# Encoder trunk on one core: norm and rotation of q and k for both token tiles at once on paired PSUM banks, key copies by DMA, attention-weight copies on ScalarE, the first norm in a set order

## The chip, the core and the metric

The kernel runs on one core of one Trainium2 chip. The metric is the device time in microseconds (us), a median over runs; less is better. TensorE (PE) does matmuls and transposes, VectorE (DVE) and ScalarE (ACT) work elementwise and read PSUM, GpSimd (POOL) does small elementwise work on SBUF, SyncE (SP) issues DMAs.

## The reference

Two layers of an encoder trunk on 256 tokens of 1024 channels, float32. Each layer projects the normed input once to the q, k, v of four mixers and four gates, mixes, and runs a convolutional feed-forward block:

```python
for l in range(DEPTH):                                   # DEPTH = 2
    h = rms_norm(x, norm1_g[l])
    aq, ak, av, bq, bk, bv, cq, ck, cv, dq, dk, dv, g = split_parts(h @ w_in[l])   # 12544 columns
    aq = rope(rms_norm(aq, gq[0, 0]), ang_1d)            # per head of 64: norm, gain, rotation
    ak = rope(rms_norm(ak, gq[0, 1]), ang_1d)
    o_a = diff_attention(aq, ak, av, ...)                # A: differential, dense
    ...                                                  # B: grouped queries, axial rotation
    ...                                                  # C: three dilated windows, 1-D rotation
    dq = rms_norm(dq, gq[3, 0]); dk = rms_norm(dk, gq[3, 1])
    o_d = neighbourhood_attention(dq, dk, dv, rpb[l])    # D: with position bias, no rotation
    merged = sum(gate[:, :, i] * (o_i @ w_branch[l, i]) for i, o_i in enumerate(mixers))
    x = x + merged @ w_out[l]
    x = x + conv_ffn(rms_norm(x, norm2_g[l]), w_up[l], conv_w[l], conv_b[l], w_down[l])
```

## The kernel before

The 256 tokens are two tiles of 128 partitions, t = 0 and 1. Weights stream in as jobs of 1 MB (`load`, L261, on SP's queue, three jobs ahead). `split` makes each half job a high and a low part: ScalarE casts (`hi`, L272), VectorE subtracts (`lo`, L273). A product is three matmuls (L346 to L348: hi x hTh, lo x hTh, hi x hTl; L342 to L344 with the weights stationary), so that two parts of the activations (`hTh`, `hTl`) and of the weights give nearly float32.

A block of 512 output columns is two jobs; a block of `branch` and the smaller `bkv` (kB) are one. The blocks follow a list: `qD kB kD qB kA vD qA vA gD0 kC1 kC0 qC1 bD0 gD1 vC0 qC0 qC2 bD1 kC2 vC1 vC2 gB0 bB0 ...` (q, k, v, g for gates, b for branches; A to D are the mixers). Each block holds two PSUM banks, one for each token tile, out of four buffers of the tag `mm`; a buffer is given to a later block when all that read it are done.

`run` walks through the jobs in quarters, and `at(j, q, fn)` hangs other work on quarter q of job j. All is put down as a program; the framework's scheduler then fixes each engine's order of instructions by a timeline of its own, with the earlier program place as the priority. `behind(ins)` lets what it encloses come after `ins` on the same engine.

What the change touches:

- `qk_vec` (L452 on), after the last quarter of a q or k block, once for each tile: ScalarE squares out of PSUM (L457), VectorE sums by head (L460), GpSimd adds the epsilon (L161) and takes the power -0.5 (L162), VectorE multiplies out of PSUM (L463, which frees the bank), and, except for D, rotates in SBUF (L479 twice or four times, L480, L482). The square's buffer `sq` is a single one, shared with the end of mixer A (`finish`, L677 to L682).
- `tr_k` (L758 on): transposes the keys of kA and kC0 (L488) and writes four operands, each with both partition halves, by four ScalarE copies (L767) and four VectorE subtractions (L769) for each tile. The dense scores read them at L527.
- `transp` (L601 on): transposes the weights of an attention unit (L608) and copies them out of PSUM on VectorE (L614); the weighted sum of mixer A is L646.
- `norm_vec`, `norm_tr` (L412, L420, L434, L437): the norm's scaling, its transposes and the copies to `hTh` and `hTl`.
- `neigh_bias` (L223): four bias matmuls for each tile half, fed by 16 loads of `rpb` on SP's queue in each layer.
- `first_norm` (L1118 on): x, the first weights and the gain row are loaded; TensorE runs 16 warm-up matmuls on zeros (L1143), then spreads the gain row over the partitions (L1149).
- `layouts` (L316 to L329): 18 matmuls on zeros behind the last product, whose result nothing reads.

Of the kernel before, what the change touches and what calls it, by code (L numbers as in the profile page):

```python
# [10 lines left out]
F32 = mybir.dt.float32  # L11
# [75 lines left out]
class Trunk:  # L87
# [77 lines left out]
    def prologue(self, l):  # L165
        nc = self.nc
        qkg = self.sb(self.tp, "qn", [128, 512], F32, bufs=3).rearrange("p (m k d) -> p m k d", m=4, k=2)
        nc.sync.dma_start(qkg, self.dram("qk_g", l * 512, [[0, 128], [1, 512]]))
        lam = self.sb(self.tp, "t2", [128, 512], F32, bufs=1)[:, :256].rearrange("p (a d) -> p a d", a=4)
# [113 lines left out]
    def run(self):  # L283
        for j in range(1, LOAD_AHEAD):
            self.load(j)
        for i in range(1, 3):
            self.split(i)
# [25 lines left out]
        with self.behind((self.last_mm,)):  # L313
            self.layouts()

    def layouts(self):  # L316

        z = self.sb(self.wp, "hi", [128, 1024], F32R, bufs=5)
        self.nc.gpsimd.memset(z[:].bitcast(F32), 0.0)
        b = self.sb(self.tp, "e", [128, 1024], mybir.dt.bfloat16, bufs=3)  # L320
        self.nc.gpsimd.memset(b, 0.0)
        p = self.ps("mm")
        v = z[:]
        at = lambda off, *dims: bass.AP(v.tensor, v.offset + off, [v.ap[0], *dims])
        kinds = [(z[:, :128], at(0, (1, 512))), (z[:, :128], at(8, (1, 512))), (z[:, :128], at(8, (0, 256), (1, 2))),
                 (z[:, :128], at(8, (16, 32), (1, 16))), (z[:, :128], at(0, (2, 512))), (b[:, :128], b[:, :512])]
        for w, m in kinds:
            for i in range(3):
                self.nc.tensor.matmul(p, w, m, start=i == 0, stop=i == 2)  # L329
# [55 lines left out]
    def in_block(self, l, col0, tile_major=False):  # L385
# [3 lines left out]
        def out():  # L389
            if "o" not in cell:  # L390
                cell["o"] = [self.ps("mm"), self.ps("mm")]
            return cell["o"]
# [8 lines left out]
    def norm_vec(self, t, g, ss, n):  # L401
# [7 lines left out]
        xn = self.t4([128, DM])  # L409
        for i in range(2):  # L410
            s = slice(i * 512, (i + 1) * 512)
            nc.vector.scalar_tensor_tensor(xn[:, s], self.x[:, t, s], rs[:, 0:1], g[i] if isinstance(g, list) else g[:, s], op0=ALU.mult, op1=ALU.mult)  # L412
        return xn

    def norm_tr(self, t, xn, by_token=False, halves=(0, 1)):

        for i in halves:
            p = self.ps("mm")
# [23 lines left out]
    def sumsq(self, t, cols, ss, i, vector=False):  # L442
        junk = self.sb(self.tp, "t2" if vector else "sq", [128, 512], F32, bufs=1)
# [8 lines left out]
    def qk_vec(self, p, t, m, k, nh, res):  # L452
# [3 lines left out]
        sq = self.sb(self.tp, "sq", [128, 512], F32, bufs=1)  # L456
        nc.scalar.activation(sq[:, :w], p[:, :w], AF.Square, scale=0.125)  # L457
        rs = self.small("qr", 8)
        hv = lambda a: a.rearrange("p (h d) -> p h d", d=64)
        nc.vector.tensor_reduce(rs[:, :nh], hv(sq[:, :w]), AX.X, ALU.add)  # L460
        self.rsqrt_mean(rs[:, :nh], rs[:, :nh], nh)
        qn = self.sb(self.tp, "qn", [128, 512], F32, bufs=3)
        nc.vector.tensor_tensor(hv(qn[:, :w]), hv(p[:, :w]), rs[:, :nh].unsqueeze(2).to_broadcast([128, nh, 64]), ALU.mult)  # L463
        if m == MD:
            if k == 1:
                nc.vector.tensor_tensor(hv(qn[:, :w]), hv(qn[:, :w]),
                                        self.dtab.unsqueeze(1).to_broadcast([128, nh, 64]), ALU.mult)
        else:
            t2 = self.sb(self.tp, "t2", [128, 512], F32, bufs=1)
            hw = 16 if m == MB else 32  # L470
            rv = lambda a: a.rearrange("p (h b w) -> p h b w", b=2, w=hw)
            tv = lambda a: a.rearrange("p (a b w) -> p a b w", b=2, w=hw)
            na = 64 // (2 * hw)
            for a in range(na):
                for b in range(2):
                    o = t2[:, :w].rearrange("p (h a b w) -> p h a b w", a=na, b=2, w=hw)[:, :, a, b, :]
                    i = qn[:, :w].rearrange("p (h a b w) -> p h a b w", a=na, b=2, w=hw)[:, :, a, 1 - b, :]
                    sv = tv(self.tab[:, m, k, 1, t, :])[:, a, b, :]
                    nc.vector.tensor_tensor(o, i, sv.unsqueeze(1).to_broadcast([128, nh, hw]), ALU.mult)  # L479
            nc.vector.tensor_tensor(hv(qn[:, :w]), hv(qn[:, :w]),  # L480
                                    self.tab[:, m, k, 0, t, :].unsqueeze(1).to_broadcast([128, nh, 64]), ALU.mult)
            nc.vector.tensor_tensor(qn[:, :w], qn[:, :w], t2[:, :w], ALU.add)  # L482
        res[t] = qn
# [7 lines left out]
    def qk_transpose(self, res, t, dst, m, k):  # L491
        nc = self.nc
        qn = res[t]
        if m == MB and k == 1:

            p = self.ps("tp")
            dup = self.sb(self.tp, "t2", [128, 512], F32, bufs=1)
# [102 lines left out]
    def transp(self, u):  # L600
# [13 lines left out]
        nc.vector.tensor_copy(pt[:, :n * 128], p[:, :n * 128])  # L614
# [46 lines left out]
    def finish(self, u, o):  # L661
# [11 lines left out]
        if m == MA:  # L673

            nc.vector.reciprocal(r[:, :4], sums.rearrange("p (h c) -> p h c", c=2)[:, :, 0])
            sq = self.sb(self.tp, "sq", [128, 512], F32, bufs=1)
# [38 lines left out]
    def layer(self, l):  # L715
# [6 lines left out]
        def start():  # L722
# [3 lines left out]
            self.prologue(l)  # L726
# [8 lines left out]
        def qk(m, k, c, col0, tile_major=False):  # L735
# [5 lines left out]
            def vec(t):  # L741
                self.qk_vec(cell["o"][t], t, m, k, 8, res)
# [456 lines left out]
```

## Time and profile before

| | |
|---|---|
| median of 3 runs | 1252.45 us (1250.09 to 1255.32) |
| profiled execution | 1251.69 us, of it 1249.9 us span |
| PE busy | 1228.6 us, 98% |
| DVE busy | 945.4 us, 76% |
| ACT busy | 703.9 us, 56% |
| POOL busy | 134.6 us, 11% |
| mean granted TensorE clock | 0.992 |
| DMA | 207.89 MB, mean 166 GB/s |

The span runs from the first to the last instruction of the profiled execution; the time of an execution holds a little more. Busy time says how long an engine worked, not who was waited for: that is read from the waits of an engine, from the chain of work that ended last, and from the order of single instructions around a wait. A wait stands in brackets behind the instruction that waited, with the one that released it.

### The profile page before, as it was taken

Reading aid. Unit: us, or ns where it says so; the run is one execution under the profiler, and the core shown is the slowest. Engines: PE = TensorE matmul, PEld = TensorE weight load, DVE = VectorE, ACT = ScalarE, POOL = GpSimd, SP = SyncE. Lnnn points to the kernel's source line nnn. Section 1 sums busy time; section 2 is a strip of 40 time slices with the busy share of each in tenths; the row PEclk is TensorE's granted clock in tenths of the full one; section 3 lists DMA queues with packets and bytes.
Section 4 is the critical chain, followed back from the end, with each engine's and each line's share of the span. In section 5 each row is a group of like instructions: output and inputs, shape, how many; then the busy total and the mean of one; then the engine's idle time right before and its main releaser. Section 6 shows DMA issues by size and latency. Waiting matters only on the chain.

```text
span 1249.9 us, 18980 instructions
## 1 busy us (share of the span) xinstructions
PE 1228.6 (98%) x7417; PEld 1052.5 (84%) x7418; DVE 945.4 (76%) x1579; ACT 703.9 (56%) x1159; POOL 134.6 (11%) x122
## 2 busy tenths in 40 slices
PE   7999999989999999999999999999899999999999
PEld 5888888878888889998878888888688888999987
DVE  6898799895555679887478988979665656888853
ACT  3557766536444457665355867755544343767641
POOL 1321130420000000000023112204200000000000
PEclk8999999989999999999999999999999999999999
DMA  8655435354346645665545454354344443666551
GB/s 239 214 184 174 136 136 170 134 176 156 123 147 163 197 144 194 196 208 203 195 166 178 147 190 136 109 195 169 122 148 155 135 161 109 203 202 203 191 183 64
DMA packets 126390, 207.89 MB, mean 166 GB/s; under 512 B 8829, under 2 KB 56541, under 8 KB 126302
## 3 DMA queue, kind: packets, MB, share of 16 engines
q1 hardware_dynamic: 125756, 205.64, 49.9%
q8 instruction: 58, 0.95, 0.3%
q10 hardware_dynamic: 546, 1.05, 0.3%
q14 instruction: 30, 0.25, 0.1%
HBM read 203.53 MB, written 1.05 MB: 164 GB/s over the span
## 4 chain that ended last, share of the span: by engine, by line
PE 88%; DVE 5%; POOL 2%; DMA 2%; issue 1%; SPq 1%; ACT 1%; ACTq 0%; DVEq 0%
PE mm L346 16%; PE mm L347 16%; PE mm L348 16%; PE mm L344 6%; PE mm L342 6%; PE mm L343 6%; PE tp L608 2%; PE tp L348 2%; PE tp L346 2%; PE tp L347 2%; DVE lo L273 2%; PE o L632 1%; PE tp L488 1%; PE s L527 1%; PE s L549 1%
## 5 line engine op out<-in xcount | busy, mean ns | idle before, releaser
L273 DVE TENSOR_TENSOR lo<-w,hi 128x1024 fp32r<-128x1024 f32 x376 | 456.7, 1220 | 188.4 <-ACT hi L272 187.0
L272 ACT CAST hi<-w 128x1024 fp32r<-128x1024 f32 x376 | 391.8, 1051 | 295.9 <-PE mm L348 169.8
L346 PE MATMUL mm<-hi,hTh 128*128 128x512 f32 (+1 forms) x800 | 315.5, 396 | 9.1 <-DVE qn L463 8.5
L347 PE MATMUL mm<-lo,hTh 128*128 128x512 f32 (+1 forms) x800 | 314.6, 394 | 0.9 <-DVE lo L273 0.9
L348 PE MATMUL mm<-hi,hTl 128*128 128x512 f32 (+1 forms) x800 | 313.3, 393 | 0.0
L342 PE MATMUL mm<-hTh,hi 128*128 128x256 f32 x704 | 193.8, 276 | 1.2 <-ACT hTh L434 1.2
L344 PE MATMUL mm<-hTl,hi 128*128 128x256 f32 x704 | 194.0, 276 | 0.9 <-DVE hTl L437 0.5
L343 PE MATMUL mm<-hTh,lo 128*128 128x256 f32 x704 | 194.1, 276 | 0.0
L346 PEld LDWEIGHTS mm<-hi,hTh 128*128 128x128 f32 x800 | 151.8, 190 | 39.6 <-issue 8.9
L347 PEld LDWEIGHTS mm<-lo,hTh 128*128 128x128 f32 x800 | 151.8, 190 | 30.6 <-DVE lo L273 1.6
L348 PEld LDWEIGHTS mm<-hi,hTl 128*128 128x128 f32 x800 | 151.5, 190 | 30.2 <-DVE hTl L437 1.1
L342 PEld LDWEIGHTS mm<-hTh,hi 128*128 128x128 f32 x704 | 131.9, 188 | 1.7 <-ACT hTh L434 1.7
L344 PEld LDWEIGHTS mm<-hTl,hi 128*128 128x128 f32 x704 | 132.0, 188 | 1.3 <-DVE hTl L437 0.7
L343 PEld LDWEIGHTS mm<-hTh,lo 128*128 128x128 f32 x704 | 132.2, 188 | 0.0
L162 POOL TENSOR_TENSOR sm_qr<-sm_qr,mhalf 128x8 f32<-128x8 f32 (+1 forms) x48 | 88.4, 1842 | 4.0
L346 PE MATMUL mm<-hi,t 128*128 128x512 f32 (+1 forms) x192 | 74.6, 388 | 0.0
L348 PE MATMUL mm<-hi,t 128*128 128x512 f32 (+1 forms) x192 | 74.0, 387 | 0.0
L347 PE MATMUL mm<-lo,t 128*128 128x512 f32 (+1 forms) x192 | 73.7, 384 | 0.0
L1032 ACT ACTIVATE e<-mm,cwT 128x256 f32<-128x256 f32 x88 | 47.1, 560 | 27.9 <-PE mm L344 25.4
L408 POOL TENSOR_TENSOR sm_nr<-sm_nr,mhalf 128x1 f32<-128x1 f32 x8 | 4.4, 551 | 537.8 <-DVE sm_nr L405 529.1
L161 POOL TENSOR_SCALAR sm_qr<-sm_qr 128x8 f32<-128x8 f32 (+1 forms) x48 | 30.0, 624 | 253.3 <-DVE sm_qr L460 251.7
L1033 DVE SCALAR_TENSOR_TENSOR e<-mm,cwT,e 128x255 f32<-128x255 f32 x88 | 39.5, 476 | 12.0 <-ACT e L1032 11.9
(177 smaller groups left out, 1698.9 us busy)
## 6 DMA issues: line engine op xcount, KB each, us to landing
w<-in_w_in_dram SPq DMA_DIRECT2D x97, 1024.0 KB, 5.1
w<-in_w_up_dram SPq DMA_DIRECT2D x44, 1024.0 KB, 5.0
w<-in_w_down_dram SPq DMA_DIRECT2D x22, 1024.0 KB, 4.9
w<-in_w_branch_dram SPq DMA_DIRECT2D x16, 1024.0 KB, 5.0
w<-in_w_out_dram SPq DMA_DIRECT2D x8, 1024.0 KB, 5.1
t<-t SPq DMA_DIRECT2D x32, 64.0 KB, 2.0
t<-in_rpb_dram SPq DMA_DIRECT2D x32, 62.5 KB, 4.8
t<-in_norm_g_dram SPq DMA_DIRECT2D x3, 512.0 KB, 6.6
```

Of the source, the lines that this page charges most:

```text
L161: nc.gpsimd.tensor_scalar(dst, ss, EPS, None, op0=ALU.add)
L162: nc.gpsimd.tensor_tensor(dst, dst, self.mhalf[:, :n], ALU.pow)
L272: self.nc.scalar.copy(hi, w)
L273: self.last_split = self.nc.vector.tensor_tensor(lo, w, hi[:].bitcast(F32), ALU.subtract).ins
L342: mm(out, wh, xh, start=first, stop=False)
L343: mm(out, wl, xh, start=False, stop=False)
L344: mm(out, wh, xl, start=False, stop=last)
L346: mm(out, xh, wh, start=first, stop=False)
L347: mm(out, xh, wl, start=False, stop=False)
L348: self.last_mm = mm(out, xl, wh, start=False, stop=last).ins
L1032: nc.scalar.activation(y[:, b:b + 256], o[:, b:b + 256], AF.Identity, scale=cw(1, z), bias=cw(3, z))
L1033: nc.vector.scalar_tensor_tensor(y[:, b + 1:b + 256], o[:, b:b + 255], cw(0, z), y[:, b + 1:b + 256], op0=ALU.mult, op1=ALU.add)
```

## The change

PSUM: the tag `mm` becomes two buffers of two banks each, `mm2()`; a block takes one pair, tile t in half t. `norm_tr`, the output projection and the up projection take their banks out of such pairs as well. `qk_vec` works on a pair: squares, sums and powers for each tile, all later steps once for both, over twice the columns. `tr_k` copies and subtracts each half once, and at the second tile GpSimd issues four DMAs that copy the halves to the other partitions. The weight copies of L614 go to ScalarE. In `first_norm` the loads change queues, the gain matmuls stand inside the warm-up, and sums, scaling, splits and transposes of the first tile follow one another in a set order ahead of the second tile; the prologue comes behind the second tile's scaling. `layouts` is gone.

```diff
     def ps(self, tag, shape=(128, 512)):
-        bufs = {"mm": 4, "s": 1, "tp": 2, "o": 1}[tag]
+        bufs = {"s": 1, "tp": 2, "o": 1}[tag]
...
+    def mm2(self):
+        return self.pp.tile([128, 2, 512], F32, tag="mm", name=self.name("mm"), bufs=2)
+
+    def pair(self, cell):
+        cell["p"] = self.mm2()
+        cell["o"] = [cell["p"][:, t] for t in range(2)]
...
     def run(self):
-        for j in range(1, LOAD_AHEAD):
-            self.load(j)
-        for i in range(1, 3):
-            self.split(i)
...
-        with self.behind((self.last_mm,)):
-            self.layouts()
...
-    def qk_vec(self, p, t, m, k, nh, res):
+    def qk_vec(self, p2, m, k, nh, res):
         nc = self.nc
         w = nh * 64
-        sq = self.sb(self.tp, "sq", [128, 512], F32, bufs=1)
-        nc.scalar.activation(sq[:, :w], p[:, :w], AF.Square, scale=0.125)
-        rs = self.small("qr", 8)
+        p = p2[:, :, :w]
+        sq = self.sb(self.tp, "sq", [128, 2, 512], F32, bufs=1)
+        rs = self.small("qr", 16)[:, :2 * nh].rearrange("p (t h) -> p t h", t=2)
         hv = lambda a: a.rearrange("p (h d) -> p h d", d=64)
-        nc.vector.tensor_reduce(rs[:, :nh], hv(sq[:, :w]), AX.X, ALU.add)
-        self.rsqrt_mean(rs[:, :nh], rs[:, :nh], nh)
-        qn = self.sb(self.tp, "qn", [128, 512], F32, bufs=3)
-        nc.vector.tensor_tensor(hv(qn[:, :w]), hv(p[:, :w]), rs[:, :nh].unsqueeze(2).to_broadcast([128, nh, 64]), ALU.mult)
+        for t in range(2):
+            nc.scalar.activation(sq[:, t, :w], p[:, t], AF.Square, scale=0.125)
+            nc.vector.tensor_reduce(rs[:, t], hv(sq[:, t, :w]), AX.X, ALU.add)
+            self.rsqrt_mean(rs[:, t], rs[:, t], nh)
+        qn2 = self.sb(self.tp, "qn", [128, 2, 512], F32, bufs=2)
+        qn = qn2[:, :, :w]
+        th = lambda a: a.rearrange("p t (h d) -> p t h d", d=64)
+        nc.vector.tensor_tensor(th(qn), th(p), rs.unsqueeze(3).to_broadcast([128, 2, nh, 64]), ALU.mult)
...
+            nc.vector.tensor_tensor(th(qn), th(qn), self.tab[:, m, k, 0].unsqueeze(2).to_broadcast([128, 2, nh, 64]), ALU.mult)
+            nc.vector.tensor_tensor(qn, qn, t2, ALU.add)
...
-        nc.vector.tensor_copy(pt[:, :n * 128], p[:, :n * 128])
+        nc.scalar.copy(pt[:, :n * 128], p[:, :n * 128])
...
+            with self.behind((self.first_xn,) if l == 0 else (self.last_split,)):
+                self.prologue(l)
...
                 p = self.head_transpose(res[t])
-                for i in range(2):
-                    r = slice(64 * i, 64 * i + 64)
-                    hi, lo = stt[m]["ks"][i], stt[m]["ks"][2 + i]
-                    for j in range(2):
-                        nc.scalar.copy(half(hi[64 * j:64 * j + 64], t), four(p[r]))
-                    for j in range(2):
-                        nc.vector.tensor_tensor(half(lo[64 * j:64 * j + 64], t), four(p[r]), half(hi[r], t).bitcast(F32), ALU.subtract)
+                self.evac_split([(four(p[64 * i:64 * i + 64]), *(half(ks[j + i][64 * i:64 * i + 64], t) for j in (0, 2))) for i in range(2)])
+                if t == 1:
+                    for j in range(4):
+                        r = slice(64 * (j % 2), 64 * (j % 2) + 64)
+                        nc.gpsimd.dma_start(ks[j][64 - r.start:128 - r.start], ks[j][r])
...
         nc.sync.dma_start(*xrows(0))
         nc.scalar.dma_start(*xrows(1))
-        nc.sync.dma_start(*part(0, 1))
-        nc.scalar.dma_start(row, self.dram("norm1_g", 0, [[DM, 1], [1, DM]]))
-        nc.scalar.dma_start(*part(1, 1))
+        nc.scalar.dma_start(*part(0, 1))
+        nc.sync.dma_start(row, self.dram("norm1_g", 0, [[DM, 1], [1, DM]]))
+        nc.sync.dma_start(*part(1, 1))
...
+        g = [self.ps("tp") for i in range(2)]
+        for i in range(15):
+            if i in (8, 9):
+                last = nc.tensor.matmul(g[i - 8], ones, row[:, (i - 8) * 512:(i - 7) * 512], start=True, stop=True).ins
+                continue
+            with self.behind((last,) if i else None):
+                last = nc.tensor.matmul(p, zero[:, :128], zero[:, :512], start=True, stop=True).ins
...
+        def between(xn):
+            nonlocal last
+            with self.behind((self.last_xn,)):
+                self.split(0)
+            with self.behind((self.last_split,)):
+                last = self.norm_tr(0, xn, halves=(0,))
+            return last
+
+        xn = self.norm_vec(0, g, sums(0), 2, between)
+        with self.behind(last):
+            self.split(1)
+        with self.behind((self.last_split,)):
+            last = self.norm_tr(0, xn, halves=(1,))
+        with self.behind(last):
+            self.split(2)
+            xn1 = self.norm_vec(1, g, sums(1), 2)
+        self.first_xn = self.last_xn
```

## Rows read from the trace of the kernel before

**Rows 1.** The page: busy us, share of the span and instructions of each engine.

```profile
PE 1228.6 (98%) x7417; PEld 1052.5 (84%) x7418; DVE 945.4 (76%) x1579; ACT 703.9 (56%) x1159; POOL 134.6 (11%) x122
```

**Rows 2.** TensorE's waits: line <- releaser: us in total, times, longest.

```profile
PE mm L346 <- DVE qn L463: 8.5, 2, 4.3
```

**Rows 3.** Timeline of the start: start us, us, engine, line, operation [idle before].

```profile
6.75 0.56 POOL L408 TENSOR_TENSOR sm_nr<-sm_nr,mhalf 128x1 f32<-128x1 f32 x1 [5.32 <-DVE sm_nr L405]
...
8.12 1.98 PE L1149 MATMUL mm<-t,sm_ones 1*128 1x512 f32 x4
...
12.04 0.69 DVE L446 CUSTOM_DVE_ANT_0 t<-x 128x512 f32<-128x512 f32 x1 [5.44 <-DMA x<-in_x_dram]
...
12.98 2.82 DVE L412 SCALAR_TENSOR_TENSOR t<-x,sm_nr,mm 128x512 f32<-128x512 f32 x4
```

**Rows 4.** The chain that ended last, 0 to 40: start us, us, what.

```profile
27.16 6.28 DMA t<-in_rpb_dram
...
33.48 1.10 PE tp L223 x2
```

**Rows 5.** Timelines of DVE, PE and ACT, 250 to 276, the first stall.

```profile
260.03 0.69 DVE L614 COPY pt<-tp 128x512 f32<-128x512 f32 x1
...
266.04 0.68 DVE L677 TENSOR_TENSOR t<-o,sm_rcp 128x512 f32<-128x512 f32 x1
...
264.38 1.06 PE L646 MATMUL o<-t,pt 128*128 128x128 f32 x8
...
274.88 0.77 PE L346 MATMUL mm<-hi,hTh 128*128 128x512 f32 x1 [4.25 <-DVE qn L463]
...
268.23 0.60 ACT L457 ACTIVATE sq<-mm 128x512 f32<-128x512 f32 x1
```

**Rows 6.** Windows: length, busy PE, PEld, DVE, ACT, POOL, PEclk, DMA share, GB/s.

```profile
250.00:260.00 10.00, 10.00 (x50) 8.22 (x49) 9.88 (x14) 5.37 (x6) 0.00 (x0) 1.00 0.68 225
270.00:280.00 10.00, 5.75 (x17) 4.45 (x16) 8.55 (x24) 1.54 (x2) 5.75 (x5) 0.66 0.39 131
880.00:890.00 10.00, 5.75 (x25) 4.47 (x24) 8.31 (x14) 2.96 (x5) 7.45 (x6) 0.88 0.38 131
```

**Rows 7.** Groups by line and form: count | busy us, mean ns | idle before.

```profile
L273 DVE TENSOR_TENSOR lo<-w,hi 128x1024 fp32r<-128x1024 f32 x376 | 456.7, 1220 | 188.4 <-ACT hi L272 187.0
...
L463 DVE TENSOR_TENSOR qn<-mm,sm_qr 128x512 f32<-128x512 f32 x44 | 30.1, 684 | 11.4 <-POOL sm_qr L162 9.6 <-PE tp L488 1.6
...
L614 DVE COPY pt<-tp 128x384 f32<-128x384 f32 x32 | 17.7, 553 | 6.1 <-PE tp L608 6.0
...
L614 DVE COPY pt<-tp 128x512 f32<-128x512 f32 x16 | 10.9, 684 | 1.2 <-PE tp L608 1.1
```

**Rows 8.** Single lines: count, ns min/median/max, first and last start us, forms.

```profile
L769 DVE TENSOR_TENSOR t<-tp,t x32: 676/688/696, 94.9 to 814.5; 64x512 fp32r<-64x512 f32 x32
...
L527 PE MATMUL s<-t,t x128: 274/281/388, 179.1 to 992.7; 128*128 128x256 f32 x128
...
L162 POOL TENSOR_TENSOR sm_qr<-sm_qr,mhalf x48: 715/1668/2752, 29.8 to 886.4; 128x8 f32<-128x8 f32 x44, 128x2 f32<-128x2 f32 x4
```

**Rows 9.** Timelines of PE, POOL and DVE, 651 to 655, second layer's start.

```profile
653.01 0.40 PE L346 MATMUL mm<-hi,hTh 128*128 128x512 f32 x1
...
651.47 2.75 POOL L162 TENSOR_TENSOR sm_qr<-sm_qr,mhalf 128x8 f32<-128x8 f32 x1
...
654.26 0.69 DVE L463 TENSOR_TENSOR qn<-mm,sm_qr 128x512 f32<-128x512 f32 x1 [1.57 <-POOL sm_qr L162]
```

**Rows 10.** DMA issues: out<-in, queue, operation, count, KB each, median us to landing.

```profile
t<-t SPq DMA_DIRECT2D x32, 64.0 KB, 2.0
...
out_dram<-x ACTq DMA_DIRECT2D x4, 128.0 KB, 2.8
```

**Rows 11.** Timeline of the end.

```profile
1244.30 0.69 DVE L1083 TENSOR_TENSOR x<-x,o 128x512 f32<-128x512 f32 x1 [0.67 <-PE o L348]
...
1248.41 0.59 PE L329 MATMUL mm<-e 128*128 128x512 bf16 x2
```

More of the change, by code (lines that the diff above doesn't have):

```diff
@@ L312, in run @@
                     self.split(2 * j + 4)
-        with self.behind((self.last_mm,)):
-            self.layouts()
[L316 to L329, printed above, removed]
     def behind(self, last):
@@ L398, in in_block, with norm_vec @@
         return cell
-    def norm_vec(self, t, g, ss, n):
+    def norm_vec(self, t, g, ss, n, between=None):
         nc = self.nc
@@ L409, in norm_vec @@
         xn = self.t4([128, DM])
+        after = None
         for i in range(2):
             s = slice(i * 512, (i + 1) * 512)
-            nc.vector.scalar_tensor_tensor(xn[:, s], self.x[:, t, s], rs[:, 0:1], g[i] if isinstance(g, list) else g[:, s], op0=ALU.mult, op1=ALU.mult)
+            with self.behind(after):
+                scaled = nc.vector.scalar_tensor_tensor(xn[:, s], self.x[:, t, s], rs[:, 0:1], g[i] if isinstance(g, list) else g[:, s], op0=ALU.mult, op1=ALU.mult)
+            self.last_xn = scaled.ins
+            if between and i == 0:
+                after = between(xn)
         return xn
     def norm_tr(self, t, xn, by_token=False, halves=(0, 1)):
+        if 0 in halves:
+            self.norm_p = self.mm2()
         for i in halves:
-            p = self.ps("mm")
+            p = self.norm_p[:, i]
             for k in range(4):
@@ L949, in out @@
             def out():
-                if c not in acc:
-                    acc[c] = [self.ps("mm"), self.ps("mm")]
-                    if c == 1:
-                        acc[c][1] = (acc[c][1], self.ps("o"))
+                if not acc:
+                    p = [self.mm2() for t in range(2)]
+                    acc[0] = [p[t][:, 0] for t in range(2)]
+                    acc[1] = [p[0][:, 1], (p[1][:, 1], self.ps("o"))]
                 return acc[c]
@@ L1012, in mm @@
             def mm(hl, q):
-                for c in range(2):
-                    if "o" not in cells[c]:
-                        cells[c]["o"] = self.ps("mm")
+                if "o" not in cells[0]:
+                    p2 = self.mm2()
+                    for c in range(2):
+                        cells[c]["o"] = p2[:, c]
                 hv, lv = (a.rearrange("p (k n) -> p k n", k=4) for a in hl[q // 2])
@@ L1139, in first_norm, with sums @@
             nc.sync.dma_start(*xrows(u))
+        for j in range(1, LOAD_AHEAD):
+            self.load(j)
         p = self.ps("s")
-        for i in range(16):
-            nc.tensor.matmul(p, zero[:, :128], zero[:, :512], start=True, stop=True)
         ones = self.small("ones", 128, 1)[:1]
         nc.gpsimd.memset(ones, 1.0)
-        g = [self.ps("mm") for i in range(2)]
-        for i in range(2):
-            nc.tensor.matmul(g[i], ones, row[:, i * 512:(i + 1) * 512], start=True, stop=True)
-        for t in range(2):
+        g = [self.ps("tp") for i in range(2)]
[5 more added lines that the diff above has]
+                last = nc.tensor.matmul(p, zero[:, :128], zero[:, :512], start=True, stop=True).ins
+        def sums(t):
             ss = self.small("ss", 4)
@@ L1153, in first_norm, with second @@
                 self.sumsq(t, slice(i * 512, (i + 1) * 512), ss, i, vector=i == 1)
-            xn = self.norm_vec(t, g, ss, 2)
-            if t == 0:
-                last = self.norm_tr(0, xn, halves=(0,))
-                with self.behind(last):
-                    self.split(0)
-                self.norm_tr(0, xn, halves=(1,))
-            else:
-                def second():
-                    with self.behind((self.last_mm,)):
-                        self.norm_tr(1, xn)
-                self.at(0, 1, second)
+            return ss
+        last = None
+        def between(xn):
[3 more added lines that the diff above has]
+            with self.behind((self.last_split,)):
+                last = self.norm_tr(0, xn, halves=(0,))
+            return last
[8 more added lines that the diff above has]
+        self.first_xn = self.last_xn
+        def second():
+            with self.behind((self.last_mm,)):
+                self.norm_tr(1, xn1)
+        self.at(0, 1, second)
 def trunk_kernel(tc, d):
```

48 lines of the change are left out of this document (21 added, 27 removed).

## The prediction

> **What bounds the kernel now.** I read the page's busy times first: TensorE works 1228.6 us of a span of 1249.9 [rows 1], so a change that takes no matmul away can give back only the time in which TensorE stands, runs at the lower clock, or lies outside the products. I then asked who ends TensorE's waits. Apart from the start, the one large entry is a product that waits for line 463, the multiply by which VectorE reads a q/k result out of PSUM: 8.5 us in two waits [rows 2]. So the stages that matter are the start, the two stalls (one in each layer), and the tail.
>
> At the start VectorE scales the first token tile (L412) only at 12.98, although the factor from GpSimd was there at 6.75 + 0.56 = 7.31 and the gain rows at 8.12 + 1.98 = 10.10. It had put the second tile's square sum first, and that waited until 12.04 for x [rows 3]. But the chain that ended last runs there through something else: through the loads of the position bias, the last of which ends at 33.44, and the bias matmul at 33.48 [rows 4].
>
> In the first stall TensorE stands 4.25 us, until 274.88, for a bank of kC2, which by the job list is the last block but one. Its square (L457) ran only at 268.23, since ScalarE does it behind the end of mixer A, which waits for VectorE's L677 at 266.04, for the weighted sum at 264.38, and for the weight copy that VectorE made at 260.03 [rows 5]. The price is more than the wait. VectorE was busy 9.88 of 10 us in 250 to 260; the granted clock averages 0.66 in 270 to 280 and 0.88 in 880 to 890 [rows 6], so for 6.8 and 2.4 us it was at 1.2 GHz instead of 2.4. Of the first, at most 280 - 274.88 = 5.1 us held work, half of it lost: 2.5 us; of the second 1.2. Both stalls together are 8.5 + 3.7 = 12.2 us.
>
> **The change, part by part.** *Start.* Sums, factor and first half of tile 0 no longer stand behind the second tile's x. The gain matmuls follow eight warm-up matmuls, so they should be done near 7.4, with the factor at 7.31: the scaling moves from 12.98 to about 7.4, 5.6 us earlier, and splits and transposes are set in the order of need. Tile 1 isn't late for that: x at 12.0, then 0.69 + 0.3 + 0.56 + 2 x 0.70, and some 2.5 us of transposes and copies give 18, when the 24 products of tile 0 (0.23 each, from about 12.5) end. What is late next is the bias: if the matmul of 33.48 keeps its place among TensorE's instructions and its load still ends at 33.44, all but TensorE's own 0.55 us of waiting is kept from gaining. The order is made new, and a TensorE that is earlier in the list should meet the bias later in it. Between 0.5 and 5.6 I take 4.0.
>
> *VectorE and ScalarE.* The 48 weight copies leave VectorE: 17.7 + 10.9 = 28.6 us; ScalarE pays at most 48 x 0.60 = 28.8, by its 512-column square [rows 5, 7]. The key blocks issue 16 instead of 32 subtractions, 16 x 0.688 = 11.0 us off VectorE [rows 8], and 16 fewer copies on ScalarE, some 9 us at the same 0.6. Pairing merges two instructions into one: 2 x 0.684 - 1.220 (the cost of 1024 columns) = 0.15 us for each merge [rows 7]; 18 rotated blocks with 5 merges and a few more make about 15 us. In all VectorE falls by some 55 of 945 us, ScalarE rises by some 20 of 704. Neither is the bound on average; only what falls in 180 to 270 and 790 to 880 counts.
>
> *The two stalls.* In the 25 us ahead of the stall VectorE loses one or two copies and about 1.5 us of merges, some 3 us; the last copy ahead of the weighted sum can run on ScalarE, busy 5.37 of 10 us there [rows 6], at about 258.5 instead of 260.7. The weighted sum, L677 and the square of kC2 follow some 5 us earlier. Against that, the pair is freed as a whole: the second tile's GpSimd power, 1.67 us in the median [rows 8], and the longer multiply, 1.22 instead of 0.69, come on top, 2.7 us with GpSimd's add. So a release at 274.7 becomes 274.7 - 5 + 2.7 = 272.4, against 270.6 when TensorE asks: near 1.8 us if kC2's square stays tied to mixer A's end, none if it doesn't. I take 1.1 left of each stall, with no lower clock: 12.2 - 2.2 = 10.0 us gained, between 12.2 gained and some 5 lost.
>
> *New waits from pairs.* kB is a block of one job with half the columns, so kD asks soon for qD's banks. In the second layer kD starts at 653.01, while the multiply of qD's second tile starts at 654.26, having waited 1.57 us for GpSimd [rows 9]; TensorE worked on the first tile meanwhile. With one pair it can't: 654.26 + 1.22 - 653.01 = 2.5 us of new standing, and about the same in the first layer. The power ran 2.75 us there against 1.67 in the median, so an undisturbed GpSimd would give over 1 us back. Between 0 and 2.5 each I take 1.5, 3.0 for two. The Trainium skill (SBUF — State Buffer, Who interferes with whom) says that a VectorE instruction with two SBUF inputs and a GpSimd one that reads SBUF exclude each other. The spread in [rows 8] fits; as merged multiplies hold longer, the rule speaks for the upper end, which would raise the sum by 2.0.
>
> *Key copies.* 16 moves of 256 KB, issued by GpSimd. No row shows a DMA of that queue. Its nearest are SBUF copies of 64 KB (2.0 us to landing), and outputs of 128 KB (2.8) [rows 10], twice which may stand for the upper end. The keys of the first block are written from 94.9 and the first dense scores run at 179.1 [rows 8], so either price is covered. Behind the waiting issue stand GpSimd's powers; a block that ends then could be freed up to some 2 us late. I take 0, and keep 2 for the range. By the Trainium skill (DMA: Bandwidth & Descriptors, Anatomy of one DMA) such a transfer would take an estimated 2.0 + 0.6 us; no run here shows it, and the sum is unchanged.
>
> *PSUM elsewhere.* In the up projection both halves of a pair must be read before it is free; that is covered by 11 us of the next pair's products. Cost 0.
>
> *Tail.* The matmuls of L329 end at 1248.41 + 0.59 = 1249.0, the last addition at 1244.99 [rows 11]. An output landing takes 2.8 us [rows 10], so without them the work ends near 1247.8: 1.2 us less.
>
> Sum: -4.0 - 10.0 + 3.0 - 1.2 = -12.2. The profiled execution took 1251.69, 1.8 over its span and 0.8 under the median of 1252.45. So 1251.69 - 12.2 = 1239.5, on the median's level 1240.2: I say 1240.
>
> **Rivals.** *The bias loads hold the start.* The lead is 0.5 instead of 4: 1243.7. For it, the chain already goes through them; against it, the order is new. *The stalls stay.* Mixer A's last weighted sum keeps its place, the merges give back just what the pair costs: -4 + 3 - 1.2 = -2.2, so 1250. For it, the square was tied to mixer A's end and not to its own block; against it, VectorE is full just there and gets lighter. *Slower: the pair holds the next block.* All four places then wait for GpSimd's second power: 2.7 us more at each of the two stalls, 2.5 at each kD, and standing of that length pulls the clock down, as the 4.25 us did, for about 2 us each. That is 5.4 + 5.0 + 8 - 4 - 1.2 = +13.2, so 1265; it decides from the point where the pair is free over 2 us after TensorE asks. For it, the late multiply of [rows 9]; against it, blocks of two jobs leave some 11 us. *The change doesn't do what it says*: the scheduler fills the queues in another order and start and stalls both remain: about 1251, counted with the stalls.
>
> **How the numbers follow.** Forecast (1240) 0.48, bias (1244) 0.18, stalls stay (1250) 0.22, slower (1265) 0.12. All gains at their ends, 5.6 + 12.2 + 1.2 and nothing lost, give 1233.5, two more if clock time at the start is won too: the low end is 1231. The high end takes in the stalls that stay with 2 to 3 us of new waits, 1253, and leaves out the slower case. A difference under 0.5% (6.3 us) can hardly be told from no change here. Faster by more: 0.48 + 0.18 and a little of the third, less what falls short: 0.66. Within: 0.24. Slower by more: 0.10.
>
> **What would show it.** In the profile after: scaling of tile 0 near 7.4 and the first products near 11; the chain at the start no longer through the bias load; no wait of TensorE for the q/k multiply above 2 us near 270 and 880, and granted clock 1.0 there; a wait of 1 to 2.5 us at the start of each kD; VectorE near 890 us, ScalarE near 720. The forecast is wrong if either stall is still there at length, or if a new wait of some us appears with the clock falling behind it.

## The result, and the profile after

The changed kernel takes 1300.2 us in the median (1296.8 to 1303.3) against 1251.7 (1250.1 to 1255.3) of the kernel before beside it: a ratio of 1.038, interval 1.035 to 1.042. It is 48 us slower; forecast were 1240, and the slower rival stood at 1265.

The page of the changed kernel: busy us, share of the span, instructions.

```profile
span 1301.5 us, 18856 instructions
PE 1246.8 (96%) x7397; PEld 1066.2 (82%) x7397; DVE 915.0 (70%) x1401; ACT 718.0 (55%) x1191; POOL 123.1 (9%) x136
```

Against [rows 1], with 20 fewer instructions, TensorE is busy 18.2 us longer, and the span less its busy time grew from 21.3 to 54.7. So of 51.6 us, 33.4 are time outside its work and 18.2 slower work. The mean granted clock fell from 0.992 to 0.978; some 4 of the 18.2 us are not the clock, but the slower rate of the up projection in the second layer that the last section shows. VectorE fell by 30 us and ScalarE rose by 14; neither shows in the time.

TensorE's waits, line <- releaser: us in total, times, longest; then one by GpSimd's queue:

```profile
PE mm L334 <- DVE qn L462: 19.4, 6, 5.7
PE mm L415 <- DVE hTl L432: 7.1, 5, 2.7
PE s L232 <- DMA t<-in_rpb_dram: 4.0, 1, 4.0
PE mm L415 <- DVE t L402: 3.6, 2, 2.2
PE mm L330 <- ACT hTh L429: 2.3, 2, 1.2
...
PE mm L330 <- DVE e L1032: 2.0, 1, 2.0
...
POOL t L765 <- ACT t L429: 45.6, 3, 17.9
```

The q/k multiply (now L462) had two waits of 8.5 us in all [rows 2]; it has six of 19.4. New are the norm's transposes (L415) that wait for the subtraction of the half before (L432), and an up product (L330) that waits for VectorE's reads (L1032). In the last line GpSimd waits to issue the key copies (L765).

The start, where [rows 3] had the scaling at 12.98:

```profile
7.58 0.75 DVE L402 SCALAR_TENSOR_TENSOR t<-x,sm_nr,tp 128x512 f32<-128x512 f32 x1 [0.74 <-POOL sm_nr L396]
...
26.39 2.03 PE L232 MATMUL s<-t,cst 128*128 128x500 f32 x2 [4.01 <-DMA t<-in_rpb_dram]
```

The scaling came where it was forecast, and the first product 4.5 us earlier (11.97). Then TensorE stood 4.01 us for the bias load, and the granted clock was 0.66 from 25 to 35.

The start of the second layer's kD, against [rows 9]. The squares and the multiply are those of qD, for whose banks kD's first product waits. Below it are qD's squares in the kernel before:

```profile
674.91 1.09 ACT L456 ACTIVATE sq<-mm 128x512 f32<-128x512 f32 x2 [0.26 <-PE mm L336]
...
678.77 1.23 DVE L282 TENSOR_TENSOR lo<-w,hi 128x1024 fp32r<-128x1024 f32 x1 [0.54 <-ACT hi L281]
...
679.00 2.54 POOL L171 TENSOR_TENSOR sm_qr<-sm_qr,mhalf 128x8 f32<-128x8 f32 x1
...
681.57 1.23 DVE L462 TENSOR_TENSOR qn<-mm,sm_qr 128x1024 f32<-128x1024 f32 x1 [0.62 <-POOL sm_qr L171]
...
682.94 0.47 PE L334 MATMUL mm<-hi,hTh 128*128 128x512 f32 x1 [2.62 <-DVE qn L462]
```

```profile
642.62 0.60 ACT L457 ACTIVATE sq<-mm 128x512 f32<-128x512 f32 x1 [3.21 <-PE mm L348]
...
648.50 0.60 ACT L457 ACTIVATE sq<-mm 128x512 f32<-128x512 f32 x1 [0.33 <-PE mm L348]
```

Before, the first tile was squared 5.9 us ahead of the second, while TensorE still worked on the second (1.5 to 11.3 us ahead over the 24 blocks). In the changed kernel both squares start only when the products of both tiles are done, in all 24 blocks at most 0.5 us apart.

The first stall of before [rows 5]; it stands at the same block, vC2, which waits for the banks of kC2:

```profile
272.52 0.59 ACT L610 COPY pt<-tp 128x512 f32<-128x512 f32 x1 [0.30 <-PE tp L604]
...
276.93 1.05 PE L642 MATMUL o<-t,pt 128*128 128x128 f32 x8
...
278.94 0.63 ACT L674 ACTIVATE sq<-t 128x512 f32<-128x512 f32 x1
...
280.41 1.08 ACT L456 ACTIVATE sq<-mm 128x512 f32<-128x512 f32 x2
...
288.55 0.77 PE L334 MATMUL mm<-hi,hTh 128*128 128x512 f32 x1 [3.68 <-DVE qn L462]
```

The stall is there, 3.68 us here and 5.7 in the second layer. The copy on ScalarE ends at 273.11, and the weighted sum runs 3.8 us later.

### The profile page after: what moved, and what is told of

It reads as the page before. It is cut to its first block, busy times and chain, and to the rows that moved or that the text cites. A ratio compares the mean times of both kernels' runs of the same rounds, so it can differ in the third digit from the quotient of the medians.

```text
span 1301.5 us, 18856 instructions
## 1 busy us (share of the span) xinstructions
PE 1246.8 (96%) x7397; PEld 1066.2 (82%) x7397; DVE 915.0 (70%) x1401; ACT 718.0 (55%) x1191; POOL 123.1 (9%) x136
## 4 chain that ended last, share of the span: by engine, by line
PE 89%; DVE 4%; ACT 2%; POOL 2%; issue 1%; DMA 1%; SPq 0%; POOLq 0%; ACTq 0%; DVEq 0%
PE mm L334 16%; PE mm L336 16%; PE mm L335 16%; PE mm L330 6%; PE mm L332 6%; PE mm L331 6%; PE tp L604 2%; PE tp L335 2%; PE tp L334 2%; PE tp L336 2%; POOL sm_qr L171 1%; PE tp L484 1%; PE o L628 1%; PE s L523 1%; DVE lo L282 1%
## 5 line engine op out<-in xcount | busy, mean ns | idle before, releaser
L282 DVE TENSOR_TENSOR lo<-w,hi 128x1024 fp32r<-128x1024 f32 x376 | 457.5, 1222 | 235.0 <-ACT hi L281 232.8
L334 PE MATMUL mm<-hi,hTh 128*128 128x512 f32 (+1 forms) x800 | 320.0, 400 | 23.7 <-DVE qn L462 19.4
L336 PE MATMUL mm<-hi,hTl 128*128 128x512 f32 (+1 forms) x800 | 316.6, 396 | 0.0
L330 PE MATMUL mm<-hTh,hi 128*128 128x256 f32 x704 | 198.6, 282 | 4.3 <-ACT hTh L429 2.3
L332 PE MATMUL mm<-hTl,hi 128*128 128x256 f32 x704 | 198.3, 282 | 0.0
L331 PE MATMUL mm<-hTh,lo 128*128 128x256 f32 x704 | 198.2, 282 | 0.0
L336 PEld LDWEIGHTS mm<-hi,hTl 128*128 128x128 f32 x800 | 152.8, 191 | 30.8 <-DVE hTl L432 0.4
L330 PEld LDWEIGHTS mm<-hTh,hi 128*128 128x128 f32 x704 | 134.3, 191 | 5.1 <-ACT hTh L429 2.9
L331 PEld LDWEIGHTS mm<-hTh,lo 128*128 128x128 f32 x704 | 135.9, 193 | 0.0
L171 POOL TENSOR_TENSOR sm_qr<-sm_qr,mhalf 128x8 f32<-128x8 f32 (+1 forms) x48 | 81.7, 1703 | 3.8
L336 PE MATMUL mm<-hi,t 128*128 128x512 f32 (+1 forms) x192 | 74.0, 387 | 0.0
L1030 DVE SCALAR_TENSOR_TENSOR e<-mm,cwT,e 128x255 f32<-128x255 f32 x88 | 42.0, 478 | 4.8 <-ACT e L1029 4.4
L1032 DVE SCALAR_TENSOR_TENSOR e<-mm,cwT,e 128x255 f32<-128x255 f32 x88 | 42.4, 483 | 2.9
```

The costliest lines, as they stand in the source:

```text
L171: nc.gpsimd.tensor_tensor(dst, dst, self.mhalf[:, :n], ALU.pow)
L282: self.last_split = self.nc.vector.tensor_tensor(lo, w, hi[:].bitcast(F32), ALU.subtract).ins
L330: mm(out, wh, xh, start=first, stop=False)
L331: mm(out, wl, xh, start=False, stop=False)
L332: mm(out, wh, xl, start=False, stop=last)
L334: mm(out, xh, wh, start=first, stop=False)
```

## The experiments

Each ran beside the kernel before on the same chip; ratios are to that.

| run | median us | before us | ratio, interval |
|---|---|---|---|
| single | 1258.4 | 1250.9 | 1.005 (1.003 to 1.007) |
| pairs_only | 1299.4 | 1250.9 | 1.037 (1.034 to 1.039) |
| pairs_merged | 1299.3 | 1250.9 | 1.037 (1.035 to 1.040) |
| after_early | 1295.9 | 1250.9 | 1.034 (1.031 to 1.037) |
| late_fin | 1238.7 | 1250.9 | 0.989 (0.987 to 0.991) |
| wcopy | 1256.6 | 1250.9 | 1.003 (1.000 to 1.005) |
| first_early | 1253.5 | 1250.9 | 1.002 (1.000 to 1.004) |
| keydma | 1244.2 | 1250.9 | 0.993 (0.990 to 0.996) |
| after_late | 1285.8 | 1253.5 | 1.027 (1.024 to 1.029) |
| after_norm | 1289.0 | 1253.5 | 1.030 (1.027 to 1.033) |
| after_all | 1280.2 | 1253.5 | 1.022 (1.020 to 1.025) |
| both | 1242.1 | 1253.5 | 0.992 (0.989 to 0.994) |
| pairs_sums_first | 1278.5 | 1254.9 | 1.019 (1.014 to 1.023) |
| after_all_up | 1279.7 | 1254.9 | 1.020 (1.016 to 1.024) |
| after_split | 1279.4 | 1251.4 | 1.023 (1.018 to 1.027) |
| after_sq2 | 1287.2 | 1251.4 | 1.028 (1.025 to 1.031) |

Executions of one kernel lie in groups 4 to 5 us apart, for which the last section has a likely reason; medians of four runs carry that much.

### Pairs, or the rest

**single**: the change without its pairs.

```diff
-        cell["p"] = self.mm2()
-        cell["o"] = [cell["p"][:, t] for t in range(2)]
+        cell["o"] = [self.ps("mm"), self.ps("mm")]
...
-                self.qk_vec(cell["p"], m, k, 8, res)
+                self.qk_vec(cell["o"][t], t, m, k, 8, res)
```

> The change with its pairs undone: four single PSUM banks, norm and rotation for each tile by itself; key copies by DMA, weight copies on ScalarE, the new first norm and the missing layouts stay. Theory (a pair is tracked as one thing, so that whoever reads one half waits for the writers of both, and whoever writes either half waits for the readers of both): the 48 us come back, apart from the second layer's tables, which stand ahead of the norm's subtraction (2.7 us of waiting and about as much again at the lower clock); with 4 gained at the start 1250, between 1242 and 1256, and the two squares of a q/k block 1.6 us or more apart again. Rival (the other parts make the loss): 1285 or more.

Of the 48 us 42 come back, but 1258.4 lies above the 1256 that were expected at most. The tables cost about what was put down for them: from the first product of qD to that of kB the second layer takes 17.8 us, where it took 12.6. The 4 us that the start was to give aren't there (kD begins 1.2 us later than before), and the profiled execution has the slower up projection of the last section in its first layer.

**pairs_only**: the kernel before, with only the pairs (below for the q/k, v and gate blocks; those of the norms, the output and the up projection are paired as in the change); **pairs_merged**: and with the merged `qk_vec`.

```diff
-        cell["o"] = [self.ps("mm"), self.ps("mm")]
+        cell["p"] = self.mm2()
+        cell["o"] = [cell["p"][:, t] for t in range(2)]
```

> The kernel before with nothing but paired tiles in PSUM; every instruction is still issued for each tile by itself. Theory (the pair is tracked as a whole): the loss is there without any merged instruction, 1292 (1282 to 1302), and the two squares of a q/k block follow each other within 0.6 us. Rival 1 (only the merged multiply holds the pair): each half is released by its own multiply, 1252 (1248 to 1257), squares 1.6 us or more apart. Rival 2 (the other parts): 1252.

> The kernel before with paired tiles and the merged norm and rotation, no other part of the change. Theory: within 6 us of the paired tiles alone, 1290; the merges give VectorE some 15 us, which is not the bound. Rival 1 (the merged multiply): 1290 here, against 1252 for the paired tiles alone. Rival 2 (the other parts): 1252.

The pairs alone cost what the whole change costs, with every instruction as before, and the merged multiply on top changes nothing (1299.3). The time is the theory's, but the squares of a q/k block lie 5.1 to 10.3 us apart, which neither theory had. The timeline of `pairs_only` at the second layer's kD:

```profile
675.49 0.60 ACT L468 ACTIVATE sq<-mm 128x512 f32<-128x512 f32 x1 [0.26 <-PE mm L357]
...
680.16 0.69 DVE L474 TENSOR_TENSOR qn<-mm,sm_qr 128x512 f32<-128x512 f32 x1 [1.89 <-POOL sm_qr L171]
...
680.95 0.60 ACT L468 ACTIVATE sq<-mm 128x512 f32<-128x512 f32 x1 [1.64 <-DVE qn L474]
...
685.63 0.69 DVE L474 TENSOR_TENSOR qn<-mm,sm_qr 128x512 f32<-128x512 f32 x1 [1.69 <-POOL sm_qr L171]
...
686.47 0.77 PE L355 MATMUL mm<-hi,hTh 128*128 128x512 f32 x1 [4.90 <-DVE qn L474]
```

These are again the squares and multiplies of qD. The first square waits for the second tile's products, and the second square, of the other half and the other bank, waits for VectorE's multiply of the first. ScalarE's waits of that kind, which neither kernel has:

```profile
ACT sq L468 <- DVE qn L474: 30.3, 17, 4.0
```

They are waits on semaphores that the framework set. The rows read as if it took the pair for one thing and kept all that different engines do to it in the order in which it was written down, readers behind readers too; the next run tests that. By the Trainium skill (PSUM — Partial Sum Buffer, PSUM bank collisions raise a hardware error) two different engines must not touch the same bank and quadrant of partitions at once, even both reading, while different banks are free. So the rule explains an order within a bank; here the trace shows it across two. No run lets both engines at the two halves unguarded, so what the chip would do isn't shown.

**pairs_sums_first**: `pairs_only`, with another order.

```diff
-            self.at(J(e), 3, lambda: vec(0))
-            self.at(J(e), 3, lambda: vec(1))
+            def vec():
+                rs = [self.qk_sums(cell["o"][t], 8) for t in range(2)]   # square, sum, power
+                for t in range(2):
+                    self.qk_vec(cell["o"][t], t, m, k, 8, res, rs[t])    # multiply, rotate
+            self.at(J(e), 3, vec)
```

(The squares have two buffers `sq` there instead of one, which is a second edit.)

> The kernel before with paired tiles and instructions for each tile (as in the run of the paired tiles alone, 1299.4), but both tiles' squares, sums and powers are written down ahead of the two multiplies. Theory (accesses of different engines to a pair keep the order in which they are written down, even where both only read, and read different halves): the second square no longer waits for the first multiply and follows the first within 0.7 us; the waits of 4.9 us at kD shrink to 2.4 to 3.4 us, with some of the lower clock behind them: 1294 (1289 to 1298). Rival (only the release of the pair as a whole counts, and the readers are free): squares 5 us and more apart as before, 1299.

Its timeline at the second layer's kD:

```profile
658.82 1.09 ACT L468 ACTIVATE sq<-mm 128x512 f32<-128x512 f32 x2 [0.26 <-PE mm L357]
...
662.53 0.69 DVE L481 TENSOR_TENSOR qn<-mm,sm_qr 128x512 f32<-128x512 f32 x1 [0.40 <-POOL sm_qr L171]
...
664.78 0.68 DVE L481 TENSOR_TENSOR qn<-mm,sm_qr 128x512 f32<-128x512 f32 x1
...
665.61 0.47 PE L355 MATMUL mm<-hi,hTh 128*128 128x512 f32 x1 [0.94 <-DVE qn L481]
```

The squares moved together (in 20 of 24 blocks at most 0.5 us apart), no square waits for a multiply any more, the wait at kD fell from 4.90 to 0.94, and the gain was 21 us, not 5. So the order of the readers is shown as the cause of these waits. The 21 us are not shown to be the order's alone: no run gave this kernel the second buffer by itself, and in the changed kernel that buffer gave 13 us (`after_sq2`, below). By vA, the eighth block, `pairs_only` lags the kernel before by 12.9 us and this kernel by 2.0; in the changed kernel the second buffer brought the lag there from 6.8 to 2.8, so most of the difference is likely the order's. What is left over before, 24 to 28 us, builds up mostly elsewhere: at the first products of its blocks this kernel lags 1.2 us at kD and 4.5 at gC1 in the first layer, then 6.5 at the first up block and 10.4 at the second layer's qD.

### What holds the pair in the changed kernel

**after_split**: the changed kernel, norm and rotation issued for each tile in the order just shown, with two buffers for `sq`; **after_sq2**: the merged form, only `bufs=2` for `sq`.

> The changed kernel with pairs, but norm and rotation issued for each tile by itself: both tiles' squares, sums and powers first, then the two multiplies; two buffers for the squares. Theory (the merged multiply holds the whole pair until the second power, and is longer): 1283 (1275 to 1290), waits at kD of about 1 us instead of 2.5. Rival (merged or not is the same on a pair, and the gain of the sums written first came from the order of that one program): 1297 or more.

> The changed kernel with merged norm and rotation, and only two buffers for the squares instead of one. Theory (the squares of kC2 stand behind mixer A's end in ScalarE's order, whatever buffer they write): nothing, 1297 or more. Rival (the single buffer ties them): the waits of 3.7 and 5.7 us for kC2's pair go, 1289 or less.

The second buffer alone gives 13 us, against my theory. Yet its kC2 squares (274.34) still follow mixer A's (273.81). The weighted sum comes 5 us earlier than in the changed kernel (271.80 against 276.93), and the wait for kC2's pair is 0.94 instead of 3.68. Whether the buffer or the new order did it, the run doesn't tell. On top of it the split gives 8 us; its wait at kD is 0.94, against 2.62 in the changed kernel and 2.94 in `after_sq2`. So the merged multiply holds the pair, but is the smaller part.

**after_norm**: the transposes of the later norms in the single banks `tp`.

```diff
-            p = self.norm_p[:, i]
+            p = self.ps("tp")
```

> The changed kernel, but the transposes of the second norm and of the second layer's first norm go to two single banks (those of the head transposes), one for each half, instead of a pair. Theory (the second half's transposes wait for the first half's subtraction only because the two lie in one pair): these waits, 2 to 3.8 us in each of three places, and part of the lower clock go, 1292 (1287 to 1296). Rival (VectorE is late with the norm anyway): 1298 or more.

It took back 11 us. It also leaves both pairs to the products, which the run doesn't tell apart. The changed kernel's second-layer start shows the wait that was meant:

```profile
655.86 0.69 DVE L432 TENSOR_TENSOR hTl<-mm,hTh 128x512 fp32r<-128x512 f32 x1 [0.36 <-ACT hTh L429]
...
656.60 0.66 PE L415 MATMUL mm<-ident,t 128*128 128x128 f32 x4
...
662.68 0.22 DVE L191 SCALAR_TENSOR_TENSOR tab<-cst,qn 128x64 f32<-128x64 f32 x1
...
667.16 0.67 DVE L432 TENSOR_TENSOR hTl<-mm,hTh 128x512 fp32r<-128x512 f32 x1
...
667.89 1.12 PE L415 MATMUL mm<-ident,t 128*128 128x128 f32 x4 [2.70 <-DVE hTl L432]
```

Each second half is transposed right after the first half's subtraction (656.60 after 656.55, 667.89 after 667.83). The last of these stands behind the prologue, 36 table instructions from 662.68 to 666.8, which the change tied there.

**after_early**: that tie taken away in the second layer.

```diff
-            with self.behind((self.first_xn,) if l == 0 else (self.last_split,)):
+            with self.behind((self.first_xn,) if l == 0 else None):
```

> The changed kernel, but the second layer's prologue (36 small table instructions on VectorE) isn't tied behind a split, so that it may run early as it did before. Theory: takes away the wait of 2.7 us near 665 and part of the lower clock behind it: 1295 (1292 to 1298). Rival (the tables hold up more than that one wait): 1288 or less. Second rival (whatever is done, the pair's own waits move into the place): 1300.

4.3 us, as expected. That is no more than the groups of the executions, but it shows where it should: from the first product of qD to that of kB the second layer takes 14.7 us, against 18.9 in the changed kernel.

### The stalls of the kernel before

**late_fin**: the kernel before, mixer A's last end behind kC2's norm.

```diff
+            if m == MA and t == 1:
+                self.at(u["late"], 0, lambda: self.finish(u, o))   # u["late"] = J(35)
+            else:
                 self.finish(u, o)
```

> The kernel before, with the end of mixer A's last unit (scaling, square, norm) written down one block later, behind the norm of kC2. Theory (the stall of 4.25 us comes from kC2's square standing behind mixer A's end on ScalarE, which in turn stands where TensorE's own order puts the last weighted sum): the square comes right after kC2's products, both stalls go with the lower clock behind them, 8.5 + 3.7 us: 1239 (1236 to 1244). Rival (the square is late anyway, through VectorE or GpSimd): 1250.

12.2 us, the prediction's own price of the two stalls:

```profile
254.77 0.60 ACT L457 ACTIVATE sq<-mm 128x512 f32<-128x512 f32 x1
```

The square of kC2 runs here instead of at 268.23, and no wait for L463 is left. From vC1 to gB0 the blocks gain 6.8 us in the first layer and 6.0 in the second. This kernel is the fastest of all kernels here, 4.7% under the changed one.

**wcopy**: only the weight copies on ScalarE.

```diff
-        nc.vector.tensor_copy(pt[:, :n * 128], p[:, :n * 128])
+        nc.scalar.copy(pt[:, :n * 128], p[:, :n * 128])
```

> The kernel before, with only the attention-weight copies moved from VectorE to ScalarE. The prediction's step (the copy is what the last weighted sum of mixer A waits for, so it and kC2's square come some 5 us earlier): stalls near 270 and 882 shrink to 0 to 2 us, 1240 to 1245. Theory now (the weighted sum stands at its place in TensorE's order and waits for no copy): stalls of 4.2 us stay, 1251 (1249 to 1256).

Its timeline around the first stall:

```profile
260.75 0.59 ACT L614 COPY pt<-tp 128x512 f32<-128x512 f32 x1
...
265.38 1.05 PE L646 MATMUL o<-t,pt 128*128 128x128 f32 x8
...
275.27 0.47 PE L346 MATMUL mm<-hi,hTh 128*128 128x512 f32 x1 [2.87 <-DVE qn L463]
```

No gain: the weighted sum comes 4 us behind the copy and waits for nothing; it stands at its place among TensorE's products. A part of the wait moved to another block (four waits of 9.5 us, where there were two of 8.5).

**keydma**: only the key copies by DMA. **both**: with the later end, and without `layouts`.

> The kernel before, with only the key copies by DMA, issued by GpSimd. Theory (scores come long after, and no power that decides stands behind the waiting issue): 1251 (1249 to 1256). Rival (powers behind the issue come late, so that a block's banks come late): waits of TensorE for the q/k multiply of 2 us or more after a key block, 1255 or more.

> The kernel before with mixer A's end behind kC2's norm, the key copies by DMA, and without the matmuls behind the last product. Theory (what the key copies gave was the same stall, moved by another order): nothing on top of the later end but the tail's 1 us, 1238 (1235 to 1240). Rival (the key copies take work from VectorE that counts elsewhere): 1233 or less.

The key copies gave 6.6 us, expected was nothing: both stalls are gone. Their program puts mixer A's last weighted sum at 258.33 instead of 264.38. With the later end they add nothing (1242.1 against 1238.7), so it was the same stall, moved by another order. The profiles fit that better than the medians: those of `keydma` (1244.4) and `both` (1243.8) have the slower up projection of the last section in their first layer, that of `late_fin` (1239.7) in none; less its 4.7 us all three lie between 1239 and 1240.

**first_early**: only the new start, without the second layer's tie.

> The kernel before, with only the new first norm and its order of loads; the second layer's prologue isn't tied. Theory (the bias loads give the lead back): first product 3 us earlier, a wait of some 3.7 us for the bias load behind it, kD's start within 1.5 us of before, 1251 (1249 to 1256). Rival (the lead reaches the end): 1247.

As the theory had it: the first product is 2.8 us earlier, kD 0.9 later; TensorE stands 1.9 us for the bias load and 1.7 for a split.

### How far the cures reach

**after_late** (the later end, in the changed kernel), **after_all** (with the free prologue and the norms in single banks), **after_all_up** (and the up projection's reads reordered).

> The changed kernel, with the end of mixer A's last unit written down one block later, behind the norm of kC2. Theory (the waits of 3.7 and 5.7 us for kC2's pair have the same origin as the stalls of before): they go with some of the lower clock behind them, 1290 (1285 to 1295). Rival (the pair's own chain, both squares, both powers and the long multiply, holds them): 1297 or more.

> The changed kernel with three cures at once: the second layer's prologue free, mixer A's end behind kC2's norm, the norms' transposes in single banks. Theory: their gains add up (4, 10 and 8 us), 1278 (1271 to 1284), and what is left over the kernel before comes from the start, from the waits at kD and from the first blocks of the up projection. Rival (these three hold nearly all of the loss): 1260 or less.

> The changed kernel with the three cures (1280.2), and in the up projection ScalarE's four reads of a pair are written down ahead of VectorE's eight, where they alternated by half. Theory (the same order between readers holds there): the second and third block take 10.9 to 11.6 us instead of 13.1 and 11.4 in the first layer, 1277 (1273 to 1280). Rival (the pairs of the up projection cost nothing, as the prediction had it): 1280 or more.

The later end gives 14.5 us, the norms 11, the tables 4.3; together 20, not 30. They share waits: with only the norms cured the tables still hold a product of the second layer's start for 2.61 us (L336 <- L432), and in `after_all` kD's wait in the second layer is 3.95 instead of 2.62. The reordered reads show in their stage, the first three up blocks of the first layer take 37.8 us instead of 39.9, but hardly in the total: the profiled spans are 1277.8 and 1279.1, the medians 0.5 us apart, which decides nothing.

## Why the prediction was wrong, step by step

**Reading of the bound**: right. But for some 4 us of the slower up projection, the loss is time outside work and lower clock.

**New waits from pairs, and PSUM elsewhere at cost 0**: here it failed. The waits at kD came as computed, 2.51 and 2.62 us, the upper end. GpSimd's second power took 2.54 us there instead of 1.67, and VectorE's subtraction of L282, which reads two SBUF tiles, ran from 678.77 to 680.00 beside it. The Trainium skill's rule (SBUF — State Buffer, Who interferes with whom) had spoken for that end, and fits; but the instruction beside the power is that subtraction and no merged multiply, and it was so in the kernel before (L273, 651.47 to 652.69, beside the 2.75 us of [rows 9]). The error was to take a pair as two banks that are merely freed together. It is also filled and read as one: squares no longer overlap the second tile's products, the second half's transposes wait for the first half's reader, the up projection's reads fall in a row. That is in every block, not in four places; `single` puts the pairs with the merged q/k norm at 42 us, `pairs_only` the pairs without it at 48.5, where the sum had 3.0. For the up projection it had 0: the first three blocks of the first layer take 38.1 us instead of 33.5 (469.62 to 507.71, before 451.94 to 485.43), the first of the second 14.3 instead of 11.8, some 7 us. The slower rival had the mechanism and the sign, but priced four places, 1265, and got 0.12. Its "blocks of two jobs leave some 11 us" was no cover: the chain now starts only at the end of both tiles.

**The two stalls, -10**: failed. The cause (kC2's square behind mixer A's end) and the price (12.2) were right, as `late_fin` shows. That the lighter VectorE would move it was wrong: the weighted sum of [rows 5] starts 3.66 us after the copy's end (260.72 to 264.38) without a wait in brackets, so it waited for nothing and only its place in TensorE's order counted. The row was there to be read. "Stalls stay" was the right rival.

**Start, -4.0**: failed on balance. The lead came (4.5 at the first product), and the bias load took it back, as the rival said. Without pairs kD begins 1.2 us later than before; with them 5.5.

**A part not in the sum**: the prologue tied to the last split of the layer before. Before, these tables ran at 278 to 283, under other work; the tie put them ahead of the norm's subtraction, 4.3 us.

**Tail, -1.2**: from the last product to the end of the span it was 5.63 us and is 4.77, so -0.9. **Key copies, 0**: they land after 5.7 us, the upper end taken from the outputs (twice 2.8), and nobody waits; of the GpSimd queue behind them (17.9 us held at the longest) no wait of TensorE came. By themselves they weren't worth 0, but 6.6 us (`keydma`), by an order of mixer A's end that the changed kernel doesn't have. By the Trainium skill (DMA: Bandwidth & Descriptors, Anatomy of one DMA) an estimated 2.6 us would do; the measurement decides. **VectorE, -55**: -30; the merges gave 7 (958.1 us busy in `pairs_only`, 951.4 in `pairs_merged`), not 15. It didn't matter.

How the 48 us divide: 42 are pairs with the merged q/k norm (1300.2 against `single`'s 1258.4), the rest tables, start and what the 4 to 5 us groups of the executions leave uncertain. Within the 42 the cures give norms 11, kC2's place 14.5 by mixer A's later end or 13 by a second buffer for the squares, and merged multiply 8 on top of that buffer; they were not all tried together and don't add up fully. The 13 come back with the PSUM pairs untouched. Some 7 lie in the up projection; the rest is spread and not told apart. That `pairs_only` comes out at the same total looks like chance: by vA in the first layer it lags the kernel before by 12.9 us, the changed kernel by 6.8, which loses its time later, at the tables and the second layer's start (22.3 at qD, 29.9 at kD).

## What to carry to other kernels

Before two buffers are made one so that one instruction can serve both, ask of every access whether it now waits for the other half: who writes, who reads on which engine, and in which order they are written down; the saving (7 us of VectorE) was on an engine that was no bound, the cost on the one that was. For a stall, follow the chain back until an instruction has no wait in brackets: there it is the place in its engine's order that counts, and moving that place (a few lines, 12 us) does what faster work ahead of it can't.

## What the hardware showed that was not expected

The up projection runs at one of two rates, and keeps it from one of its first blocks to the last of a layer, at full granted clock and without a gap: 10.88 or 11.31 us for a block, some 4 to 5 us for a layer. Two windows of 60 us of `single`, in its first and second layer; the last columns are the granted clock, the DMA share and GB/s:

```profile
500.00:560.00 60.00, 60.00 (x512) 60.00 (x511) 52.37 (x88) 41.10 (x66) 0.00 (x0) 1.00 0.59 191
1100.00:1160.00 60.00, 60.00 (x532) 60.00 (x531) 54.12 (x89) 41.81 (x65) 0.00 (x0) 1.00 0.60 195
```

512 matmuls against 532 in the same time. Kernels with and without pairs have it; the profile of the changed kernel has the slower rate in the second layer, that of before in none. What sets it wasn't found. It would account for executions of the kernel before near 1250.5 and 1255.5, whose mean granted clock is the same, 0.992; that isn't shown, since none of the slower ones was profiled.
